# State-space tables moved in program order: all 32 steps beside the four chunks of v

## The chip, the cores and the metric

One core of a Trainium2 chip runs the whole program. The metric is device time in microseconds (us). The kernel before was run three times: 3003.44, 3010.11 and 3009.76 us, median 3009.76 us.

The engines: PE multiplies matrices (PEld loads its weights), DVE and POOL do elementwise work, ACT does activations and copies and issues some DMAs, SP issues most DMAs. Each engine works through one queue in order.

## The reference

Two layers over 256 latent and 256 context tokens of 1024 features. Layer 0 mixes tokens with a gated MLP, layer 1 with a bidirectional diagonal state-space model; after each comes a block of product-key experts. All that matters here lies in the first 400 us, where layer 0's mixer runs:

```python
mod_x = (silu_c @ ada_w[i] + ada_b[i])                    # shift, scale, gate of each sub-layer
xn = _modulate(_rmsnorm(x, norm1_g[i]), sh1, sc1)         # the "first modulated input"
z = jax.nn.gelu(h @ w_in); u, v = jnp.split(z, 2, axis=-1)
v = _layernorm(v, ln_g, ln_b)
v = jnp.einsum("hpq,bnqhd->bnphd", w_s, v) + b_s.T[:, :, None]
return (u * v.reshape(bsz, length, D_MIX)) @ w_out
```

The state-space model of layer 1 needs tables made from its weights alone (powers of the decay times B and C). They don't depend on the tokens, and they are first read in layer 1, after about 1900 us.

## The kernel before

**The opening of layer 0.** `ada_pe(pa, f)` (L187) makes 512 columns of the modulation with 16 matmuls on two loads of 1 MB (`adaw`, two buffers); six calls give shift and scale (calls 0 to 3) and the gate (4 and 5). `start` loads the tokens. `rstd` makes the RMS norm: squares on ACT, sums on DVE, 8 small matmuls, then in `norm_end` a chain of twelve tiny DVE operations (L273 and L244 to L249) that wait for each other, 4 matmuls (L279) and a copy (L281, tile `rr`). `modulate` (L322 to L325) then writes the modulated input as a high part `hh` (ACT) and a low part `hl` (DVE), eight feature blocks one after the other.

**The chunks of v.** `gmlp` loads `cm_w_in` in chunks of 256 columns (`gww`), splits each into `gwh` (ACT) and `gwl` (POOL and DVE), and computes four chunks of v, each with 96 matmuls (L309 to L311) into four PSUM banks that Gelu (L413) empties. After each chunk it calls `vpump()`. After the fourth come `vdone` (it runs the rest of the tables, closes their memory and opens that of what follows), the layer norm of v, and the chunks of u with `wprime_units` (L554, products of the query weights with the keys) and the output product between them.

**The tables.** `s5_units` (L940) is a generator of 32 steps: eight rounds of eight groups each, four steps a round. Steps 1 and 2 belong to B: four DVE multiplications (L952, into tiles `Bd` and `tp`) and one addition (L966), 16 transposes on PE (L973), copies on ACT, two DMAs. Steps 3 and 4 belong to C: four multiplications (L952, into `Cd` and `tp`), one addition (L985), 32 matmuls (L998), copies, DMAs. `go(k)` takes k steps. `Bd` and `tp` have one buffer, `Cd` two.

**What sets the order.** The program is written once in Python; a planner puts every instruction into its engine's queue at the time at which its own model of the machine finds it ready, and among ready ones the one that was written first. So an operation written later can be pulled ahead into time in which its engine would stand idle, if its inputs and its buffers are free. `tc.issue_after(x)` puts what is written in it behind x on x's engine. PSUM banks are tiles named `bk0` to `bk7`, handed out in turn by `bank()` as the program is written; each has one buffer, so the users of a bank follow each other in program order.

The order that is written, before: tables' steps 1 and 2 after `start`; 8 steps after `modulate`; 6 steps behind `modulate`'s last DVE operation; 4 steps after each chunk of v.

Of the kernel before, what the change touches and what calls it, by code (L numbers as in the profile page):

```python
# [71 lines left out]
F1 = 4  # L72
PIN = 1
HA = 50
G_A = 2
G_B = 0
GEND = 0.97
I1 = 0
# [5 lines left out]
WU = (3, 3, 3, 2, 2, 2, 1, 0, 0)  # L84
# [12 lines left out]
AW = (0.12, 0.35)  # L97
PC_ = 1
PD_ = 0
G_C = 8  # L100
G_D = 1
HB = 0
HC = 0
HD = 0
HE = 0
# [6 lines left out]
def tile_hybrid(ctx: ExitStack, tc: tile.TileContext, I, out, stop=None):  # L112
# [11 lines left out]
    def urgent(n):  # L124

        return tc.high_priority(n) if n else ExitStack()

    def use_banks(*b):
        banks[0] = list(b)
# [6 lines left out]
    def pool(name, bufs=1, side=None):  # L136
        return tc.tile_pool(name=name, bufs=bufs, side=side, reuse_waits="tile")
# [21 lines left out]
    def start(pl):  # L159
        load(XT[:, :, 0:SEQ], I["x"].rearrange("(b p) t -> p b t", p=P))  # L160
        for b in range(0, KB, 2):
            pos = pl.tile([P, 2, SEQ], F32, name="pos", bufs=2)
            load(pos, I["pos"][b * P:(b + 2) * P, :].rearrange("(b p) t -> p b t", p=P))
            nc.vector.tensor_add(XT[:, b:b + 2, 0:SEQ], XT[:, b:b + 2, 0:SEQ], pos)
        load(XT[:, :, SEQ:T], I["ctx"].rearrange("(b p) t -> p b t", p=P))
# [3 lines left out]
    r2 = cp.tile([P, T], F32, name="r2")  # L169
# [16 lines left out]
    def ada_pe(pa, f):  # L186

        pm = bank()
        for q in range(2):
            w = pa.tile([P, 4, 512], F32, name="adaw")  # L190
            ends["ada", f] = load(w, I["ada_w0"][q * 512:(q + 1) * 512, f * 512:(f + 1) * 512].rearrange("(b p) f -> p b f", p=P)).ins
            for b in range(4):
                nc.tensor.matmul(pm[0:2, :], cT[:, 4 * q + b, :], w[:, b, :], start=(q + b == 0), stop=(q + b == 4))
        row = pa.tile([2, 512], F32, name="adar")
        nc.scalar.copy(row, pm[0:2, :])
        pm = bank()
        for j in range(4):
            nc.tensor.transpose(pm[:, 2 * j:2 * j + 2], row[:, j * P:(j + 1) * P], ident[0:2, 0:2])
        nc.vector.tensor_tensor(mod[:, 0, 4 * f:4 * f + 4, :],
                                pm[:, 0:8].rearrange("p (j t) -> p j t", t=2),  # L200
                                ab[:, 0, 4 * f:4 * f + 4].unsqueeze(2).to_broadcast([P, 4, 2]), op=OP.add)
        scale_cols(0, 4 * f, 4)
# [81 lines left out]
    def rstd(pl, t0, t1, e=nc.gpsimd):  # L284
        pm = bank()[:, :t1 - t0]
        for b in range(KB):
            norm_add(pl, pm, b, t0, t1, e)
        return norm_end(pl, pm, t1 - t0)
# [3 lines left out]
    def ne(k):  # L292
        return nc.gpsimd if NE[k] == "P" else nc.vector
# [20 lines left out]
    def modulate(pl, r, i, a, sh, parts, keep=None):  # L314

        base, end = parts[0][1], parts[-1][2]
        for b in range(KB):
            u = pl.tile([P, end - base], F32, name="mu", bufs=2)
            for c, t0, t1, hh, hl in parts:
                x = u[:, t0 - base:t1 - base]  # L320
                bias = mod[:, i, sh + b, c:c + 1]
                nc.vector.scalar_tensor_tensor(x, XT[:, b, t0:t1], a[:, i, b, c:c + 1], r[:, t0 - base:t1 - base],  # L322
                                               op0=OP.mult, op1=OP.mult)
                nc.scalar.activation(hh[:, b], x, AF.Identity, bias=bias)
                end_ = nc.vector.scalar_tensor_tensor(hl[:, b], x, bias, hh[:, b].bitcast(F32), op0=OP.add, op1=OP.subtract)  # L325
                if keep is not None:
                    keep(b, c, t0, x, bias)
        return end_.ins
# [923 lines left out]
    def layer0():  # L1252
        n = NDENSE
        low = ExitStack()
        p1 = low.enter_context(pool("h1", side="right"))
        hh1 = p1.tile([P, KB, T], F32R, name="hh1")
        hl1 = p1.tile([P, KB, T], F32R, name="hl1")
# [3 lines left out]
        gw = gws.enter_context(pool("gw", GWB))  # L1261
        with pool("ada0", ADA0) as pa, pool("n1") as pn:
            ada_pe(pa, 0)
            with pool("s5s", side="right") as sm:
                tabs = s5_setup(s5p, sm)
            tables = s5_units(tail.enter_context(pool("s5w", 2, side="right")), *tabs)

            def go(k):
                for _ in range(k):
                    next(tables, None)  # L1270

            ada_pe(pa, 1)
            start(pn)
            go(G_A)
            ada_pe(pa, 2)
            go(G_B)
            with urgent(HA):
                r = rstd(pn, 0, T, ne(0))
            ada_pe(pa, 3)
            with urgent(HB):  # L1280
                end_ = modulate(pn, r, 0, A1, SH1, [(c, t0, t1, hh1[:, :, t0:t1], hl1[:, :, t0:t1]) for c, t0, t1 in PARTS])
            with tc.issue_after(ends["norm"]) if AF_ else ExitStack():
                ada_pe(pa, 4)
                ada_pe(pa, 5)
            go(G_C)
            with tc.issue_after(end_) if G_D else ExitStack():
                go(16 - G_A - G_B - G_C)
        units = []
        ada = []

        def vdone(st):
# [4 lines left out]
            ada.append(ada_rows(pa, [(0, f) for f in range(24, 40)] + LATE[:NP], ada_silu(pa)))  # L1296

        use_banks(*range(7))
        gmlp(gw, hh1, hl1, r2, lambda: go(4), vdone, lambda k: [next(units[0], None) for _ in range(WU[k])], low.close,
             lambda k: [next(g, None) for g in ada for _ in range(k)])  # L1300
        gws.close()
        drain(chain(*ada))
# [3 lines left out]
        with pool("hx") as ph, pool("hold", side="right") as pk, ExitStack() as hold:  # L1306
# [12 lines left out]
            with pool("hc") as pc:  # L1319
# [5 lines left out]
                with pool("n2", side="right") as pn:  # L1325
# [12 lines left out]

                    with urgent(HC):
                        modulate(pn, r2, 0, A2, SH2,  # L1340
# [53 lines left out]
    def layer1():  # L1394
# [20 lines left out]
        with pool("hx1") as ph:  # L1415
# [20 lines left out]
            with pool("de1", 2) as pd, ExitStack() as rs:  # L1436
# [59 lines left out]
                use_banks(*range(8))  # L1496

    layer0()
    if stop in ("gmlp", "peer0"):
        return dump(XT)  # L1500
# [64 lines left out]
```

## Time and profile before

| | |
|---|---|
| median of three runs | 3009.76 us |
| profiled execution, its own time | 2998.49 us |
| its span, first to last instruction | 2996.7 us |
| PE, DVE, ACT, POOL busy | 89%, 77%, 44%, 48% |
| mean granted PE clock | 0.951 |

The profiled execution was 11 us shorter than the median; a span is its own time less 1.8 us. Rows of a timeline give start, duration, engine, line, operation, tiles and count; merged rows give the whole duration of their count. What stands in brackets at the end is the time for which the engine stood idle before, and what released it.

### The profile page before, as it was taken

The numbers are of one execution on the slowest core, as the hardware profiler recorded it, in microseconds if no ns is written. First come the engines' busy times: TensorE is split into PE (matmuls) and PEld (weight loads), VectorE is DVE, ScalarE is ACT, GpSimd is POOL, SyncE is SP. The second block draws the span as 40 slices with busy tenths as digits, with TensorE's granted clock in tenths as the row PEclk, the third lists the DMA queues.
The fourth block names the chain that finished last, engine by engine and source line by source line (L and its number), as shares of the span: only waits on it lengthen the run. The fifth ranks groups of instructions, "written<-read, shape, count | busy, mean of one in ns | idle before, by whom it ended". The sixth has DMA issues, their size and how long they took to land.

```text
span 2996.7 us, 46002 instructions
## 1 busy us (share of the span) xinstructions
PE 2678.1 (89%) x16231; PEld 2375.2 (79%) x16231; DVE 2306.5 (77%) x3980; ACT 1307.0 (44%) x2412; POOL 1438.1 (48%) x1008
## 2 busy tenths in 40 slices
PE   6799899888878888999999987998788889999998
PEld 2599798888766666888888866798787888899997
DVE  7796879999977886999999986464899876644344
ACT  4553243354562233333333323334345665555554
POOL 2031134544634344788888871235454335544443
PEclk8899999999988999999999998999899999999999
DMA  8579743565658787898999987997366778866662
GB/s 276 156 241 338 258 152 123 179 223 191 228 201 268 266 295 255 310 319 311 326 305 316 312 271 253 332 342 204 113 197 232 284 266 297 275 213 216 204 208 104
DMA packets 414576, 738.89 MB, mean 247 GB/s; under 512 B 41604, under 2 KB 272260, under 8 KB 409224
## 3 DMA queue, kind: packets, MB, share of 16 engines
q1 hardware_dynamic: 310240, 507.84, 51.1%
q0 software_dynamic: 36864, 134.23, 13.1%
q10 hardware_dynamic: 67240, 93.88, 8.8%
q8 instruction: 127, 2.08, 0.3%
q14 instruction: 105, 0.86, 0.1%
HBM read 633.07 MB, written 102.77 MB: 246 GB/s over the span
## 4 chain that ended last, share of the span: by engine, by line
PE 31%; DMA 13%; DVE 11%; issue 7%; POOL 5%; ACT 1%; SPq 1%; DVEq 0%; ACTq 0%; POOLq 0%
PE bk L756 6%; PE bk L757 5%; PE bk L755 5%; PE bk L311 4%; PE bk L309 4%; PE bk L310 4%; DMA vr<-peer_v 3%; DMA row<-peer_v,ids 2%; POOL row L601 2%; DMA row<-peer_u,ids 2%; DVE ul L303 1%; POOL ul L303 1%; POOL vl L303 1%; PE bk L554 1%; SPq L134 1%
## 5 line engine op out<-in xcount | busy, mean ns | idle before, releaser
L311 PE MATMUL bk<-hxh,ul 128*128 128x384 f32 (+1 forms) x2048 | 649.5, 318 | 47.7 <-DVE ul L303 28.5
L309 PE MATMUL bk<-hxh,uh 128*128 128x384 f32 (+1 forms) x2048 | 649.6, 317 | 11.7 <-ACT uh L301 6.9
L310 PE MATMUL bk<-hxl,uh 128*128 128x384 f32 (+1 forms) x2048 | 643.8, 314 | 0.0
L303 POOL TENSOR_TENSOR ul<-ur,uh 128x512 fp32r<-128x512 f32 x299 | 447.1, 1501 | 301.9 <-ACT uh L301 268.7
L303 POOL TENSOR_TENSOR vl<-vr,vh 128x512 fp32r<-128x512 f32 x256 | 363.0, 1422 | 461.1 <-ACT vh L301 454.6
L756 PE MATMUL bk<-vl,wh 128*128 128x512 f32 x1280 | 517.8, 405 | 63.6 <-POOL vl L303 46.1
L755 PE MATMUL bk<-vh,wh 128*128 128x512 f32 x1280 | 511.5, 400 | 36.8 <-ACT wh L301 19.5
L301 ACT ACTIVATE vh<-vr 128x512 fp32r<-128x512 f32 x512 | 315.4, 623 | 519.2 <-DMA vr<-peer_v 375.9
L757 PE MATMUL bk<-vh,wl 128*128 128x512 f32 x1280 | 509.0, 398 | 0.0
L301 ACT ACTIVATE uh<-ur 128x512 fp32r<-128x512 f32 x512 | 315.5, 629 | 408.4 <-PE bk L310 226.6
L311 PEld LDWEIGHTS bk<-hxh,ul 128*128 128x128 f32 x2048 | 397.5, 194 | 55.5 <-DVE ul L303 33.8
L309 PEld LDWEIGHTS bk<-hxh,uh 128*128 128x128 f32 x2048 | 398.3, 194 | 18.9 <-ACT uh L301 7.9
L310 PEld LDWEIGHTS bk<-hxl,uh 128*128 128x128 f32 x2048 | 398.2, 194 | 5.0
L303 DVE TENSOR_TENSOR wl<-w,wh 128x384 fp32r<-128x384 f32 (+1 forms) x256 | 192.6, 753 | 242.0 <-ACT wh L301 241.4
L756 PEld LDWEIGHTS bk<-vl,wh 128*128 128x128 f32 x1280 | 246.8, 193 | 135.3 <-POOL vl L303 62.4
L755 PEld LDWEIGHTS bk<-vh,wh 128*128 128x128 f32 x1280 | 246.5, 193 | 92.0 <-ACT vh L301 22.7
L757 PEld LDWEIGHTS bk<-vh,wl 128*128 128x128 f32 x1280 | 247.1, 193 | 50.7 <-DVE wl L303 0.3
L303 DVE TENSOR_TENSOR vl<-vr,vh 128x512 fp32r<-128x512 f32 x256 | 205.2, 812 | 74.4 <-ACT vh L301 73.5
L624 DVE SCALAR_TENSOR_TENSOR acc<-row,wts,acc 128x1024 f32<-128x1024 f32 x127 | 208.3, 1640 | 21.2 <-DMA row<-peer_v,ids 20.1
L611 DVE SCALAR_TENSOR_TENSOR gscr<-row,hn 128x1024 f16<-128x1024 f32 x128 | 209.7, 1639 | 18.3 <-DMA row<-peer_u,ids 17.1
L303 DVE TENSOR_TENSOR ul<-ur,uh 128x512 fp32r<-128x512 f32 x213 | 188.7, 888 | 43.5 <-ACT uh L301 41.7
L223 DVE SCALAR_TENSOR_TENSOR adasv<-adatv,cB 128x1024 f16<-128x1024 f32 x112 | 157.3, 1405 | 61.0 <-DMA adatv<-ada_t 60.1
(325 smaller groups left out, 4966.1 us busy)
## 6 DMA issues: line engine op xcount, KB each, us to landing
ur<-peer_ut SPq DMA_DIRECT2D x256, 512.0 KB
vr<-peer_v SPq DMA_DIRECT2D x256, 512.0 KB
gd<-Gs ACTq DMA_DIRECT2D x40, 1024.0 KB
adatv<-ada_t SPq DMA_DIRECT2D x72, 512.0 KB
wqT<-peer_w_q SPq DMA_DIRECT2D x64, 512.0 KB
Gr<-gd SPq DMA_DIRECT2D x120, 192.0 KB
wp<-wpo ACTq DMA_DIRECT2D x32, 512.0 KB
wpi<-wp SPq DMA_DIRECT2D x16, 1024.0 KB
```

Source lines behind the costliest of these rows:

```text
L223: e.scalar_tensor_tensor(scr, w, 1.0, cB[:, t], op0=OP.mult, op1=OP.mult, accum_out=mod[:, i, f, t:t + 1])
L301: nc.scalar.activation(hi, src, AF.Copy)
L303: return e.tensor_tensor(lo, src, hi.bitcast(F32), op=OP.subtract)
L309: nc.tensor.matmul(o, ah, bh, start=(i == 0), stop=False)
L310: nc.tensor.matmul(o, ah, bl, start=False, stop=False)
L311: last = nc.tensor.matmul(o, al, bh, start=False, stop=(i == n - 1))
L601: tc.keep_in_program_order(nc.gpsimd.indirect_dma_start(out=r[:], out_offset=None, in_=I[f"peer_{table}{i}"], in_offset=bass.IndirectOffse ...
L611: nc.vector.scalar_tensor_tensor(scr, r, 1.0, hn, op0=OP.mult, op1=OP.mult, accum_out=dots[:, h, k:k + 1])
L624: nc.vector.scalar_tensor_tensor(acc, r, w, acc, op0=OP.mult, op1=OP.add)
L755: nc.tensor.matmul(o, wh[:, js], vh, start=first, stop=False)
L756: nc.tensor.matmul(o, wh[:, js], vl, start=False, stop=False)
L757: nc.tensor.matmul(o, wl[:, js], vh, start=False, stop=last)
```

## The change

The constants take all steps out of the opening, and `vpump()` takes eight steps instead of four. The block behind `modulate`'s last operation stays but takes none.

```diff
-G_A = 2
+G_A = 0
 G_B = 0
...
-G_C = 8
+G_C = 0
 G_D = 1
 HB = 0
+NT0 = 0
...
             go(G_C)
             with tc.issue_after(end_) if G_D else ExitStack():
-                go(16 - G_A - G_B - G_C)
+                go(NT0)
...
-        gmlp(gw, hh1, hl1, r2, lambda: go(4), vdone, ...
+        gmlp(gw, hh1, hl1, r2, lambda: go(8), vdone, ...
```

The number of steps (32) and what each computes stay the same. Since `bank()` counts on as the program is written, the opening and the first chunk get other banks than before: round 0's B transposes now use bk4, bk5, bk6 and bk0, and the first chunk of v uses bk0 to bk3. From the end of the tables on the banks are the same as before.

## Rows read from the trace of the kernel before

**Rows 1.** The page, its first line.
```profile
span 2996.7 us, 46002 instructions
```

**Rows 2.** Windows: us, busy us of PE, PEld, DVE, ACT, POOL, clock, DMA share, GB/s.
```profile
36.00:48.00 12.00, 7.90 (x32) 3.27 (x32) 11.58 (x10) 7.06 (x16) 6.75 (x4) 0.86 1.06 345
...
37.40:199.70 162.30, 129.44 (x825) 99.50 (x826) 145.60 (x145) 82.38 (x196) 31.67 (x15) 0.88 0.63 196
...
103.00:112.00 9.00, 2.42 (x12) 2.43 (x13) 8.93 (x8) 2.38 (x6) 0.00 (x0) 0.50 0.62 164
...
128.10:198.70 70.60, 69.43 (x560) 67.68 (x560) 66.94 (x49) 40.94 (x96) 17.63 (x9) 0.98 0.60 181
...
206.10:361.00 154.90, 154.49 (x962) 136.60 (x960) 112.10 (x215) 44.93 (x80) 29.14 (x19) 1.00 0.91 313
```

**Rows 3.** Table operations on DVE: count, ns min/median/max, first and last start.
```profile
L952 DVE TENSOR_TENSOR tp<-c,YC x16: 1201/1218/1226, 56.5 to 195.7; 128x1024 f32<-128x1024 f32 x16
...
L966 DVE TENSOR_TENSOR Bd<-Bd,tp x8: 2279/2292/3272, 50.9 to 192.2; 128x2048 f32<-128x2048 f32 x8
```

**Rows 4.** Timeline of DVE, from the first table operation to the last.
```profile
37.45 2.35 DVE L952 TENSOR_TENSOR Bd<-b,YB 128x1024 f32<-128x1024 f32 x2
...
41.99 8.90 DVE L952 TENSOR_TENSOR Cd<-c,YC 128x1024 f32<-128x1024 f32 x4
50.81 0.15 DVE L273 TENSOR_SCALAR dr<-bk 128x4 f32<-128x4 f32 x1
50.88 3.27 DVE L966 TENSOR_TENSOR Bd<-Bd,tp 128x2048 f32<-128x2048 f32 x1
...
73.05 2.36 DVE L952 TENSOR_TENSOR tp<-b,YB 128x1024 f32<-128x1024 f32 x2
...
75.90 0.16 DVE L249 SCALAR_TENSOR_TENSOR vr<-yr,vr 128x4 f32<-128x4 f32 x1
85.31 1.67 DVE L322 SCALAR_TENSOR_TENSOR mu<-XT,A,rr 128x256 f32<-128x256 f32 x4 [9.24 <-ACT rr L281]
...
100.03 2.35 DVE L952 TENSOR_TENSOR Bd<-b,YB 128x1024 f32<-128x1024 f32 x2
102.30 0.48 DVE L325 SCALAR_TENSOR_TENSOR hl<-mu,mod,hh 128x256 fp32r<-128x256 f32 x1
...
187.66 4.55 DVE L952 TENSOR_TENSOR Bd<-b,YB 128x1024 f32<-128x1024 f32 x2
...
197.51 2.28 DVE L985 TENSOR_TENSOR Cd<-Cd,tp 128x2048 f32<-128x2048 f32 x1
```

**Rows 5.** Timeline of SP's DMA queue, around 31 us.
```profile
31.00 0.50 SPq L134 DMA_DIRECT2D b<-s_b  x1
...
33.43 2.18 SPq L134 DMA_DIRECT2D gww<-cm_w_in  x2
```

**Rows 6.** Timeline of PE: chunk 0 of v, and the end of the tables.
```profile
58.34 2.15 PE L193 MATMUL bk<-adaw,cT 128*2 128x512 f32 x3 [0.46 <-ACT BTq L975]
...
83.49 1.16 PE L279 MATMUL bk<-ident,vr 128*128 128x128 f32 x8
...
109.58 3.67 PE L973 MATMUL bk<-ident,Bd 128*128 128x128 f32 x16 [10.00 <-DVE Bd L966]
114.39 5.77 PE L998 MATMUL bk<-Cd,bdg 128*48 128x144 f32 x32 [1.14 <-DVE Cd L985]
...
128.13 0.58 PE L309 MATMUL bk<-gwh,hh 128*128 128x256 f32 x1 [4.93 <-ACT BTq L975]
...
198.81 1.91 PE L973 MATMUL bk<-ident,Bd 128*128 128x128 f32 x16
200.65 4.12 PE L998 MATMUL bk<-Cd,bdg 128*48 128x144 f32 x32
204.71 1.98 PE L420 MATMUL bk<-wsT,ones 128*128 128x512 f32 x4
...
217.73 0.61 PE L554 MATMUL bk<-kT,wqT 128*128 128x128 f32 x4
```

More of the change, by code (lines that the diff above doesn't have):

```diff
@@ L1298, in layer0 @@
         use_banks(*range(7))
-        gmlp(gw, hh1, hl1, r2, lambda: go(4), vdone, lambda k: [next(units[0], None) for _ in range(WU[k])], low.close,
+        gmlp(gw, hh1, hl1, r2, lambda: go(8), vdone, lambda k: [next(units[0], None) for _ in range(WU[k])], low.close,
              lambda k: [next(g, None) for g in ada for _ in range(k)])
```

## The prediction

> **What bounds the kernel now.** I read the summary first, for the span [rows 1], then windows of the opening [rows 2], because the change touches nothing behind it. Two stages stand out. From 206.1 to 361.0 us PE is busy 154.49 of 154.90 us at full clock: whatever ends this stage earlier or later is PE's own work, and the stage begins when the tables are done (chunk 0 of u, then the first product L554 at 217.73 [rows 6]). Ahead of it, from the first table operation at 37.45 to the end of the last at 199.7 (197.51 + 2.28 [rows 4]), DVE is busy 145.6 of 162.3 us [rows 2]. So DVE is what carries the opening: 16.7 us of idle time is all that a better order could take out of it. PE idles more there, but for DVE: it waits 10.00 us for `Bd` at 109.58, and starts chunk 0 of v only at 128.13, although the last piece of its input was written at 102.8 (102.30 + 0.48) [rows 4, 6]. This is the gap at which the change aims, and the first thing to see is that PE isn't the engine that is late there.
>
> **The change part by part.**
>
> *The work itself.* A B half of a round is four multiplications (two back to back take 2.35 us [rows 4]) and one addition (2.29 [rows 3]), together 7.0 us; a C half is the same. A round costs 14.0 us, eight rounds 112 us. None of it goes away. PE needs 1.91 + 4.12 us a round and about 11.6 us a chunk of v (an estimate: a chunk has as many columns as chunk 0 of u, which runs from 206.1 to 217.7 [rows 2, 6]), so 23.7 us for a chunk with its two rounds, under DVE's 28. DVE stays the bound.
>
> *What can still be pulled ahead.* The planner may pull tables ahead of chunk 0 as it does now. What stops it is PSUM: a bank's users follow each other as written. That this holds shows at 58.34: call 3 of `ada_pe` waited for `BTq`, the copy that empties bk4 from round 0's transposes [rows 6]. With the new count round 0's fourth transposes use bk0, which chunk 0 of v holds first. Until that is emptied `Bd` stays taken, so no more than this runs early: round 0 (14.0 us), the first two multiplications of round 1's C (2.35) and the two of its B that go to `tp` (2.35), 18.7 us. Before, rounds 0 and 1 and four multiplications of round 2 (at 73.05 and 100.03) had run by 102.8: 28.0 + 4.7 = 32.7 us. So 14.0 us of tables move from before the modulated input to behind it.
>
> *When the modulated input is ready.* The weights of chunks 0 and 1 of v (two DMAs of 1 MB) now stand ahead of the loads of B and C, which SP issued first before [rows 5]. At 345 GB/s [rows 2] that is 6.1 us; `Bd` began at 37.45 for another reason (its table was being made), so I take 4.5 of 0 to 6.1: tables begin at 42.0. The chain of the norm begins at 50.81 behind eight multiplications and ends at 76.1, since the planner puts table operations between its tiny ones [rows 4]. I assume that it does so again with what is left: 18.7 us, plus 5.2 for operations beside POOL's splits (four multiplications took 8.90 instead of 4.7, one addition 3.27 instead of 2.29 [rows 3, 4]), plus twelve links at 0.2 (2.4), plus some 2.5 for DVE's share of the splits and modulation: 42.0 + 28.8 = 70.8. PE's broadcast (1.16 [rows 6]) and the copy add 1.8 if PE isn't behind a load, as it was before (it finished at 84.65, 8.6 us after the chain). `modulate` took 17.5 us with two table multiplications inside, so 15.1 without. Ready at 87.7 instead of 102.8.
>
> *From there to the end of the tables.* Before: 199.7 - 102.8 = 96.9 us. Added: the 14.0 moved; a hand-over in which DVE has nothing, since chunk 0 must end, be emptied, and round 0's last transposes follow before `Bd` is free (nearest row: PE's 4.93 us wait for such a copy [rows 6]; bounds 2 to 12, the upper one a whole chunk; I take 5); one more chunk's split by POOL beside DVE, for chunk 1 of u, whose buffer now comes free earlier (two multiplications took 4.55 instead of 2.35, at 187.66; twice that is 4.4). Taken away: DVE's waits between 128.1 and 198.7, 70.6 - 66.94 = 3.7 us, because PE there was full with one round a chunk, and now has slack. Sum 116.6, so the tables end at 204.3, 4.6 us later than before.
>
> *The hand-over to PE's stage.* Before, from 199.7 to the first product at 217.7, PE ran 4.1 of round 7's products, 1.4 of L420 and 11.6 of chunk 0 of u. Chunk 3 of v is now done long before, so L420 and the first half of u (5.8; its bank is free once round 7's B is copied) run while DVE makes the last C. That gives back 7.2 us (bounds 0 to 13; the second half's bank waits for round 7's C). What follows is PE's gapless 143 us with its loads released by the same tables.
>
> *The sum.* +4.6 - 7.2 = -2.6 us at 361, and nothing behind hides or multiplies it. On the profiled execution's own time (span plus 1.8) that is 2995.9; that execution lies 11.3 us under the median of the three runs, so against the median: 3009.8 - 2.6 = 3007 us. A single measurement of this kernel can't tell less than 0.3% (9 us) from no change; so this is no change, with a slight lean to faster.
>
> **The rivals.**
>
> *The chain runs ahead (faster).* If B and C land so late that the planner puts the norm's chain in front of the tables, the modulated input is ready near 75 and DVE's idle time shrinks. For it: the chain alone costs 2.4 us, and the tables start later than before, while the sums under the chain don't depend on them. Against it: the planner fills every gap of a chain with whatever is ready [rows 4]. The gain is bounded by DVE: begun at 42.0 with 145.6 of work and 4.4 more of collision, without a gap, the tables end at 192.0, 7.7 earlier; with the 7.2 of PE's hand-over, 14.9, and 19 if B and C land as early as before. I take 17: 2993 us.
>
> *PE makes DVE wait (slower).* The one mechanism that ends on the other side: in PE's queue the transposes of a round stand behind a chunk of v that was written earlier, and `Bd` has one buffer. From Bd's addition on DVE has the C half (7.0) and two multiplications (2.35) to do, 9.3 us; PE needs a chunk and the transposes, 11.6 + 1.9 = 13.5. Each chunk that falls so costs 4.2 us, four cost 17. For it: chunk 0 certainly falls so, and PE made DVE wait before too [rows 2]. Against: only some banks couple, and a chunk may also fall into DVE's C half. It decides the sign from two such chunks on. 3007 + 16 = 3023 us.
>
> *The clock (slower).* Between 103 and 112 us PE worked 2.42 of 9.00 us, the granted clock was 0.50 (the level of 1.2 GHz), and 16 transposes then took 3.67 us against 1.91 at full clock; 32 products took 5.77 against 4.12 [rows 2, 6]. With the new order PE works about 23.7 of 33 us. If it fell to the lower level in every stage, a chunk would take 23.2 and two rounds 18.9, 42.1 us against DVE's 28 + 5; 9 us too many in each of four stages, of which the first is covered, so +27: 3034 us. Against it: the low stretch followed a wait of 10 us, and the waits to come are shorter; over the whole opening PE was busy 129.44 of 162.3 us, in uneven pieces, and the clock was 0.88 [rows 2]. The Trainium skill has the rule for it ("TensorE: Matmul & The Clock Gate", section "HAM oscillation — how this bites in real kernels"): a PE that waits between bursts drops to the lower clock and pays at each burst anew; the window at 103 to 112 agrees, and by the rule alone this rival would be the forecast, at 3034.
>
> *It doesn't do what it says.* The planner pulls the same operations ahead in another order, and all stays: 3010 us. Against it are the banks; for it, that 32.7 us were pulled ahead before.
>
> **How the numbers follow.** Forecast 0.37, chain ahead 0.27, PE makes DVE wait 0.20, clock 0.08, nothing 0.08. The forecast's own range is 3007 plus or minus 9 (hand-over 2 to 12, PE's gain 0 to 13, start 0 to 6). Faster by over 0.3% (under 3000.7): most of the chain's case and a tail of the forecast, 0.30. Slower (over 3018.8): most of the two slower cases and a small tail, 0.25. Within: 0.45. The range takes in both signs: from 2990 (the chain's case with an early start) to 3026 (four chunks that make DVE wait); left out are the clock's case and the outer tails, 0.2.
>
> **What would show it.** In the profile after: the last `hl` at about 88 us instead of 102.8, with no L998 ahead of it; chunk 0 of v from about 75 to 91 instead of 128; the last L985 ending at about 204; L420 and half of u ahead of the last L998; the first L554 near 215; PE without a gap until about 358. DVE's idle time between 42 and 204 near 13 us. It is wrong if the tables end before 196 or after 212, if `hl` is written before 78 or after 97, or if the granted clock between 100 and 200 stays under 0.9.

## The result and the profile after

The changed kernel takes 3034.1 us (median of 6 runs, 3024.7 to 3043.2) where the kernel before, run beside it, takes 3010.8 (3003.4 to 3014.6): a ratio of 1.0079, 95% interval 1.0054 to 1.0103. It is slower by some 24 us; the forecast was 3007. The profiled execution took 3024.7 us. Lines of the changed kernel are one higher than before (L952 is now L953, L554 is L555).

The page's first line, and windows of the opening (columns as in [rows 2]):

```profile
span 3023.0 us, 45994 instructions
...
41.80:217.50 175.70, 127.90 (x812) 100.97 (x810) 151.58 (x160) 83.65 (x197) 38.44 (x19) 0.87 0.58 180
88.90:100.50 11.60, 11.60 (x87) 9.74 (x86) 1.59 (x6) 4.61 (x9) 0.04 (x1) 1.00 0.17 47
100.00:200.00 100.00, 76.83 (x576) 73.44 (x575) 94.32 (x73) 54.71 (x133) 19.22 (x10) 0.90 0.56 168
100.50:217.50 117.00, 84.58 (x624) 80.46 (x622) 111.32 (x95) 63.31 (x152) 27.20 (x13) 0.87 0.57 172
...
240.00:384.90 144.90, 142.70 (x908) 126.90 (x907) 105.06 (x160) 40.09 (x73) 28.33 (x18) 1.00 0.89 302
```

The first window runs from the first table operation to the last. DVE is busy 151.6 of 175.7 us there, idle 24.1, where it was busy 145.6 of 162.3 [rows 2], idle 16.7. The second window is the hole: PE is busy for all of its 11.6 us, DVE for 1.6.

DVE's timeline, to be read against [rows 4]:

```profile
41.76 3.42 DVE L953 TENSOR_TENSOR Bd<-b,YB 128x1024 f32<-128x1024 f32 x2
...
75.96 1.67 DVE L323 SCALAR_TENSOR_TENSOR mu<-XT,A,rr 128x256 f32<-128x256 f32 x4 [8.35 <-ACT rr L282]
...
87.24 1.66 DVE L326 SCALAR_TENSOR_TENSOR hl<-mu,mod,hh 128x256 fp32r<-128x256 f32 x4
94.33 0.17 DVE L200 TENSOR_TENSOR mod<-bk,ab 128x8 f32<-128x8 f32 x1 [5.43 <-PE bk L199]
...
99.84 0.69 DVE L304 TENSOR_TENSOR gwl<-gww,gwh 128x512 fp32r<-128x512 f32 x1 [4.11 <-ACT gwh L302]
100.45 3.43 DVE L953 TENSOR_TENSOR Bd<-b,YB 128x1024 f32<-128x1024 f32 x2
...
210.46 2.27 DVE L967 TENSOR_TENSOR Bd<-Bd,tp 128x2048 f32<-128x2048 f32 x1
...
212.79 2.34 DVE L953 TENSOR_TENSOR tp<-c,YC 128x1024 f32<-128x1024 f32 x2
...
215.19 2.27 DVE L986 TENSOR_TENSOR Cd<-Cd,tp 128x2048 f32<-128x2048 f32 x1
```

The last piece of the modulated input is written at 88.9 instead of 102.8, 14 us earlier, as the change means it. The next multiplication starts at 100.45, and the last table operation ends at 217.46 instead of 199.79. PE's timeline, against [rows 6]:

```profile
74.15 1.16 PE L280 MATMUL bk<-ident,vr 128*128 128x128 f32 x8
...
78.76 0.39 PE L310 MATMUL bk<-gwh,hh 128*128 128x256 f32 x1
...
98.71 1.47 PE L974 MATMUL bk<-ident,Bd 128*128 128x128 f32 x12
100.11 4.12 PE L999 MATMUL bk<-Cd,bdg 128*48 128x144 f32 x32
...
107.89 1.94 PE L974 MATMUL bk<-ident,Bd 128*128 128x128 f32 x16 [3.66 <-DVE Bd L967]
...
140.95 3.29 PE L974 MATMUL bk<-ident,Bd 128*128 128x128 f32 x16 [5.06 <-DVE Bd L967]
...
176.80 3.65 PE L974 MATMUL bk<-ident,Bd 128*128 128x128 f32 x16 [8.97 <-DVE Bd L967]
...
212.88 3.65 PE L974 MATMUL bk<-ident,Bd 128*128 128x128 f32 x16 [8.37 <-DVE ve L245]
217.41 3.78 PE L421 MATMUL bk<-wsT,ones 128*128 128x512 f32 x4 [0.89 <-ACT BTq L976]
220.21 1.42 PE L310 MATMUL bk<-hh,gwh 128*128 128x512 f32 x1
...
225.39 4.12 PE L999 MATMUL bk<-Cd,bdg 128*48 128x144 f32 x32
...
237.01 0.60 PE L555 MATMUL bk<-kT,wqT 128*128 128x128 f32 x4
239.75 0.50 PE L310 MATMUL bk<-hh,gwh 128*128 128x512 f32 x1 [2.14 <-ACT uT L376]
```

Chunk 0 of v starts at 78.8 instead of 128.1, and with its weights and input at hand PE runs it to the end at 98.9, between calls of `ada_pe`, before it transposes the other twelve blocks of round 0. From then on each second round is waited for: 3.7, 5.1, 9.0 and 8.4 us, 26.1 in all (the releaser shown for the last is a small operation behind `Bd`'s addition on DVE). So from 100.5 to the tables' end it is PE that waits for DVE: PE is busy 84.6 of 117.0 us, DVE 111.3. The first product of PE's long stage comes at 237.0 instead of 217.7, and the first product of the next norm (L267 before) at 386.5 instead of 361.7. That shift of 24.8 us is nearly the whole loss: at the end of the program it is 26.3. It has two parts: 17.7 us by which the tables end later, and 7.1 from there to the next norm (169.0 us instead of 161.9).

### The profile page after: what moved, and what is told of

Read it like the earlier page. It is cut to its first block, busy times and chain, and to the rows that moved or that the text cites. A ratio compares the mean times of both kernels' runs of the same rounds, so it can differ in the third digit from the quotient of the medians.

```text
span 3023.0 us, 45994 instructions
## 1 busy us (share of the span) xinstructions
PE 2689.2 (89%) x16231; PEld 2385.4 (79%) x16231; DVE 2305.7 (76%) x3980; ACT 1307.7 (43%) x2412; POOL 1449.9 (48%) x1008
## 4 chain that ended last, share of the span: by engine, by line
PE 28%; DMA 15%; DVE 13%; issue 7%; POOL 4%; SPq 1%; ACT 1%; DVEq 0%; ACTq 0%; POOLq 0%
PE bk L757 5%; PE bk L758 5%; PE bk L756 5%; DMA vr<-peer_v 4%; PE bk L310 4%; PE bk L312 4%; PE bk L311 4%; DMA row<-peer_v,ids 3%; POOL row L602 2%; DMA Gr<-gd 2%; SPq L135 1%; DVE ul L304 1%; DMA row<-peer_u,ids 1%; PE bk L555 1%; DVE w L742 1%
## 5 line engine op out<-in xcount | busy, mean ns | idle before, releaser
L612 DVE SCALAR_TENSOR_TENSOR gscr<-row,hn 128x1024 f16<-128x1024 f32 x128 | 201.0, 1570 | 12.3 <-DMA row<-peer_u,ids 11.1
```

The costliest lines, as they stand in the source:

```text
L612: nc.vector.scalar_tensor_tensor(scr, r, 1.0, hn, op0=OP.mult, op1=OP.mult, accum_out=dots[:, h, k:k + 1])
```

## The experiments

Theory 1: `Bd` has one buffer, and the transposes that free it stand behind a whole chunk of v in PE's queue. Theory 2, formed on the way: PE is as much the bound as DVE once chunk 0 has begun, and it is only without a gap if each chunk (11.7 us) is followed by one round (6.0), not by two. The rival to both is the forecast's own view, that DVE's work alone sets the end.

The ratios are to runs of the kernel before, made beside each on the same chip. The columns from the third on are times in us in the one profiled execution: end of the last `hl`, end of the last table operation, first product of the long stage, first product of the next norm.

| kernel | ratio to before (95%) | hl | tables | L554 | next norm |
|---|---|---|---|---|---|
| before | 1 | 102.8 | 199.8 | 217.7 | 361.7 |
| changed | 1.0079 (1.0054 to 1.0103) | 88.9 | 217.5 | 237.0 | 386.5 |
| e1, two steps behind each bank | 1.0051 (1.0032 to 1.0069) | 88.6 | 215.0 | 236.8 | 382.0 |
| e2, two Bd | 1.0004 (0.9988 to 1.0021) | 96.6 | 201.5 | 219.0 | 363.1 |
| e3, 8 ahead, held behind hl | 1.0018 (1.0007 to 1.0030) | 63.8 | 202.2 | 228.6 | 373.2 |
| e4, v's split on DVE | 1.0048 (1.0028 to 1.0068) | 81.8 | 209.1 | 230.0 | 375.9 |
| e5, before, two Bd | 0.9985 (0.9969 to 1.0002) | 103.2 | 195.9 | 217.1 | 361.6 |
| e6, before, split on DVE | 0.9943 (0.9925 to 0.9961) | 94.5 | 188.0 | 206.7 | 351.6 |
| e7, 8 ahead, free | 1.0014 (0.9999 to 1.0028) | 98.0 | 196.8 | 227.0 | 372.7 |
| e8, before, both | 0.9977 (0.9961 to 0.9994) | 106.3 | 196.2 | 218.2 | 362.7 |
| e9, 2 steps put back | 0.9993 (0.9975 to 1.0010) | 100.6 | 208.3 | 233.5 | 373.2 |
| e10, 16 held, 4 per chunk | 0.9968 (0.9947 to 0.9988) | 64.7 | 199.0 | 217.1 | 360.8 |
| e11, before, 8 per chunk | 1.0047 (1.0026 to 1.0068) | 103.7 | 198.0 | 237.5 | 384.5 |
| e12, two Bd and split | 0.9999 (0.9979 to 1.0020) | 90.6 | 200.2 | 219.8 | 373.0 |
| e13, last wait filled | 1.0057 (1.0040 to 1.0075) | 90.3 | 219.6 | 238.6 | 382.5 |
| e14, as e10, split on DVE | 0.9989 (0.9973 to 1.0005) | 62.3 | 194.3 | 212.9 | 356.4 |

The last column and the ratio go together: 3010 us times (ratio - 1), less the shift of the last column, lies between -13.6 and +2.0 in the fifteen rows, 5.5 low on average, since the profiled execution of before was one of the short ones. So a difference of 20 us in the last column is the time's; one of 5 is not told apart by the time.

**e1.** The steps spread over a chunk's banks.

```diff
-                vpump()                    # behind a chunk, go(8)
+                    vpump()                # behind each of its four banks, go(2)
```

> The changed kernel with the same 32 steps behind the chunks of v, but two of them issued after each of a chunk's four banks instead of eight after the fourth. Theory 1 (one Bd buffer, and the transposes that free it stand behind a whole chunk in PE's queue): DVE's idle time between the last hl and the next multiplication of a round falls from 11.5 us to under 4, PE's waits for Bd between the chunks (3.7, 5.1, 9.0 and 8.4 us) fall by more than half, the last L986 ends at 204 to 209 instead of 217.4, and the time falls by 8 to 13 us against the changed kernel, to 3021 to 3026. Rival (DVE is the bound by its own work: multiplications at half speed beside POOL and the layernorm's small operations between them; the waits only move): the last L986 ends after 214 and the time stays within 4 us of 3034.

DVE's idle time behind `hl` fell to 6.4 us, but the tables end at 215.0, only 2.5 earlier. PE's waits for `Bd` fell to 3.2 us, and it waited 10.2 for `Cd` and 10.0 for `BTq` instead. The time, 3023.2, is where theory 1 put it, but that is 0.3% under the changed kernel with intervals that overlap, and the steps that should lead there didn't come. So the place behind a whole chunk is not the cause by itself: most of the waits moved, as the rival had it.

**e2.** A second `Bd`.

```diff
-TB = dict(Bd=1, BTq=2, Cd=2, wk=2)
+TB = dict(Bd=2, BTq=2, Cd=2, wk=2)
...
-            u = pl.tile([P, end - base], F32, name="mu", bufs=2)
+            u = pl.tile([P, end - base], F32, name="mu", tag="sq" if i == 0 and a is A1 and end - base == T else "mu", bufs=2)
...
-            r = pl.tile([P, n], F32, name="rr")
+            r = pl.tile([P, n], F32, name="rr", tag="sqs" if n == T else "rr")
```

> The changed kernel with two Bd buffers instead of one (room for it is made by letting mu and rr of the first norm take the places of sq and sqs, which are dead by then). Theory 1 (single Bd): round 1's multiplications start within 3 us of the last hl instead of 11.5, DVE waits for Bd no more between the chunks, the last L986 ends at 204 to 209, time 3021 to 3026. Rival (what keeps DVE is the order of PE's queue alone: the transposes come as late as before, a second buffer is filled and then waited for too): the first wait goes but comes back a round later, last L986 after 213, time within 4 us of 3034.

DVE's timeline of e2, and PE's:

```profile
53.60 2.35 DVE L953 TENSOR_TENSOR Bd<-b,YB 128x1024 f32<-128x1024 f32 x2
...
96.14 0.47 DVE L326 SCALAR_TENSOR_TENSOR hl<-mu,mod,hh 128x256 fp32r<-128x256 f32 x1
...
102.29 3.43 DVE L953 TENSOR_TENSOR Bd<-b,YB 128x1024 f32<-128x1024 f32 x2
```

```profile
100.55 1.47 PE L974 MATMUL bk<-ident,Bd 128*128 128x128 f32 x12
101.95 4.12 PE L999 MATMUL bk<-Cd,bdg 128*48 128x144 f32 x32
106.00 1.97 PE L974 MATMUL bk<-ident,Bd 128*128 128x128 f32 x16
```

Round 0's transposes come as late as in the changed kernel (100.55), but round 1's B was begun at 53.60 in the second buffer and is transposed at 106.00 without a wait. DVE is still without table work for 5.7 us behind `hl`, more than expected, and the loss is gone all the same: tables to 201.5, time level with before. Of PE's waits for `Bd` 1.4 us are left, beside 4.8 for a C half and 10.5 for the copies into `BTq` (6.4 in the changed kernel). What the second buffer mends, by these rows, is that DVE and PE need not meet once per round.

**e3 and e7.** Eight of the 32 steps ahead of chunk 0 again, in two ways.

```diff
-NT0 = 0          # e3
+NT0 = 8
```
```diff
-G_C = 0          # e7
+G_C = 8
```

> The changed kernel with the first 8 steps (two rounds) issued ahead of chunk 0 of v, the other 24 behind chunks 0, 1 and 2, none behind chunk 3. Theory 1: the transposes of round 0 don't stand behind chunk 0, so the 11.5 us of DVE's idle time behind the last hl are gone; hl is some 4 us later, the last L986 ends at 205 to 210, and with nothing queued behind chunk 3 the time is 3018 to 3026. Rival (the place behind chunk 0 is not what costs; DVE's own work is): last L986 after 214, time within 4 us of 3034.

> The changed kernel with one of its three edits undone: 8 steps stand ahead of chunk 0 again, not held behind the last hl, and 24 behind chunks 0 to 2. Theory 1: both first rounds' transposes stand ahead of chunk 0, so DVE goes from hl to the next multiplication in under 3 us, as in the kernel before; the last L986 ends at 198 to 206 and the time is 3005 to 3014, as much as 8 ahead behind hl or better. Rival (what costs is that the tables are spread over the chunks, eight steps behind each): still over 3020.

In e3 I overlooked that this place is held behind the last `hl` (`issue_after(end_)` in the diff): no table ran ahead of `hl`, which was therefore written at 63.8, 25 us earlier than in the changed kernel, not 4 later. Both kernels have the hand-over mended (0 and 1.2 us) and the tables end at 202 and 197, about where before ended them, but the next norm begins 11 us late in both (e7's time, 3016.2, came out 2 us above what was expected, e3's, 3013.1, 5 us below): PE has the last part of chunk 3 to do when the tables are done (it ends at 215.8 and 214.3), because two rounds stand behind each of the chunks 0 to 2. That DVE's end and PE's start of the long stage come apart is what theory 2 was formed on.

**e4 and e6.** v's subtractions all on DVE, in the changed kernel and in the one before.

```diff
-                wh, wl = weights(I["cm_w_in"], f, (1, 2))
+                wh, wl = weights(I["cm_w_in"], f, (1, 0))
```

> The changed kernel with all gwl subtractions of v's chunks on DVE (split 1:0 instead of 1:1 with POOL). In the changed kernel the multiplications beside POOL's bursts take 13.7 us more than the others from 100 to 217; 11 subtractions of 0.6 us come to DVE instead. If DVE's own work sets the end of the tables, it comes 7 us earlier (near 210) and the time is 3025 to 3029. If the waits for Bd set it (theory 1), DVE only waits longer, the last L986 stays after 214, time within 4 us of 3034.

> The kernel before with all gwl subtractions of v's chunks on DVE. DVE is its bound up to 199.7 and idles 8 us after the last hl; the multiplications beside POOL's bursts take 13.2 us longer there, and 11 subtractions of 0.6 us come to DVE. If DVE's work sets the end of the tables there, 5 to 9 us faster: 2999 to 3005. Rival (POOL's bursts lie where DVE would wait for PE anyway): 3008 to 3011.

What POOL costs DVE, in the changed kernel (POOL's timeline, then DVE's beside it):

```profile
199.85 8.17 POOL L304 TENSOR_TENSOR gwl<-gww,gwh 128x512 fp32r<-128x512 f32 x4 [26.49 <-ACT gwh L302]
237.74 4.99 POOL L304 TENSOR_TENSOR gwl<-gww,gwh 128x512 fp32r<-128x512 f32 x4 [29.71 <-ACT gwh L302]
```

```profile
200.48 4.22 DVE L953 TENSOR_TENSOR Bd<-b,YB 128x1024 f32<-128x1024 f32 x2
204.63 4.48 DVE L953 TENSOR_TENSOR tp<-b,YB 128x1024 f32<-128x1024 f32 x2
```

Beside POOL's four subtractions a pair of multiplications takes 4.2 to 4.5 us instead of 2.35 [rows 4], and POOL's four take 8.17 where four with no table operation beside them take 4.99 (at 237.74). Together they take 9.3 us, from 199.85 to 209.11, nearly the 9.7 that they would take one after the other. The Trainium skill says so ("SBUF — State Buffer", section "SBUF: two separate sides"): the pair of ports that VectorE and GpSimd share is locked for a whole instruction, and the other engine waits; these rows agree. With the split on DVE the changed kernel's tables end at 209.1, as expected (its time, 3020.4, is lower than that), though 7 us of the 8.4 come from an earlier `hl`. Only 2.2 of these are a shorter chain of the norm (it ends at 64.9 instead of 67.1), without POOL's first burst beside it. The rest is PE's broadcast, which runs at 67.05 instead of 74.15: the products of `ada_pe` ahead of it in PE's queue waited 1.7 us for their weights instead of 5.2. The kernel before gains most (windows, then PE's timeline in both, e6 first, and DVE's in e6):

```profile
37.00:188.00 151.00, 124.40 (x823) 98.13 (x824) 140.16 (x158) 83.47 (x196) 7.94 (x4) 0.93 0.68 211
128.10:189.70 61.60, 61.08 (x506) 59.29 (x505) 59.25 (x58) 39.38 (x93) 8.56 (x5) 1.00 0.60 180
```

```profile
66.20 7.03 PE L193 MATMUL bk<-adaw,cT 128*2 128x512 f32 x16 [0.77 <-DMA adaw<-ada_w]
...
75.53 1.06 PE L279 MATMUL bk<-ident,vr 128*128 128x128 f32 x8
```

```profile
73.85 5.07 PE L193 MATMUL bk<-adaw,cT 128*2 128x512 f32 x8 [4.23 <-DMA adaw<-ada_w]
```

```profile
77.58 1.67 DVE L322 SCALAR_TENSOR_TENSOR mu<-XT,A,rr 128x256 f32<-128x256 f32 x4 [2.24 <-ACT rr L281]
```

In these windows of e6, DVE is busy 140.2 us up to the end of the tables instead of 145.6 with more instructions, PE is full from 128 on, and the whole stage is 11 us earlier at L554 and 10 at the next norm, more than the 5 to 9 expected. Only half of it is DVE's shorter work (5.4 us less busy); the other half is 5.9 us less idle, mostly because the broadcast runs at 75.53 instead of 83.49 [rows 6] and DVE waits 2.2 us for it instead of 9.2 [rows 4]. At 0.9943 this is the fastest of all versions.

**e5 and e8.** The same two edits in the kernel before: two `Bd`, and both together.

> The kernel before with two Bd buffers, edited as in the changed kernel with two. Theory 1 (the single Bd buffer costs where a round's transposes stand behind a chunk of v that is itself late; the kernel before had round 0 and 1 transposed ahead of the chunks): DVE idles only 8.0 us between the last hl and the end of the tables there, of which 3 to 5 us are waits for a buffer, so the gain is at most 5 us: 3003 to 3010. Rival (a second buffer helps wherever it is put, and the changed kernel with it came out level only because two things cancel): 22 us faster here too, near 2987.

> The kernel before with two Bd buffers and the subtractions of v's chunks on DVE, the candidate to beat both. If waits and work at half speed beside POOL add up: the tables end 8 to 14 us earlier than 199.7, 2996 to 3003. If PE's chunk of v and its banks take over as the bound of the stretch: within 4 us of the better of the two alone.

A second `Bd` ends the tables 3.9 us earlier there and moves L554 by 0.6: PE was full from 128 on, so an earlier end on DVE is worth nothing. The time, 3008.5, is in the range of theory 1, though DVE's idle time there was 5.5 us before (96.9 less 91.4) and not the 8.0 of the expectation. This is the control for e2: the second buffer is worth something only where one buffer holds the engines up. Both edits together do neither of what was expected and are no better than the split alone (L554 at 218.2 against 206.7): the planner fills the second buffer ahead of the modulation, the broadcast runs at 83.99 instead of 75.53, `hl` comes 12 us later than in e6, and PE waits 21.6 us for `Cd` ahead of chunk 0.

**e9.** Two of the 32 steps put back.

```diff
-G_A = 0
+G_A = 2
```

> The changed kernel with 2 of its 32 steps put back where they stood: the B half of round 0 is issued ahead of call 2 of ada_pe, all else as changed. Theory 1 (Bd stays taken until round 0's transposes, which stand behind chunk 0 of v on bank 0): these transposes now run before chunk 0, so DVE goes on with round 1 while it waits for the norm's broadcast and behind the last hl; the 11.5 us of idle time behind hl fall under 6, the last L986 ends at 205 to 211, the time falls by 6 to 12 us against the changed kernel, to 3023 to 3029. Rival (the place of round 0 is not what costs): tables end after 214, time within 4 us of 3034.

PE's timeline of e9, and DVE's:

```profile
55.31 3.68 PE L974 MATMUL bk<-ident,Bd 128*128 128x128 f32 x16 [9.85 <-DVE Bd L967]
...
91.33 0.39 PE L310 MATMUL bk<-gwh,hh 128*128 128x256 f32 x1
```

```profile
37.47 2.35 DVE L953 TENSOR_TENSOR Bd<-b,YB 128x1024 f32<-128x1024 f32 x2
...
109.33 4.02 DVE L953 TENSOR_TENSOR Cd<-c,YC 128x1024 f32<-128x1024 f32 x2 [0.47 <-PE bk L999]
```

All 16 transposes of round 0 run at 55.3, ahead of chunk 0 at 91.3, and the tables begin at 37.5 again. The tables end at 208.3, in the range expected; the 7.3 us of idle time behind `hl` are more than expected (two of the three waits are for chunk 0's copies and for weights). The time is level with before, a gain of 0.86% on the changed kernel, larger than the 13.3 us that the trace shows in its last column; with both intervals 13 us is just possible. So where round 0 stands is a part of the loss, as theory 1 had it: the tables end 9 us earlier although `hl` comes 11.7 us later, and eight steps still stand behind each chunk.

**e10 and e11.** One round per chunk in the changed kernel, two in the kernel before.

```diff
-NT0 = 0                                   # e10, on the changed kernel
+NT0 = 16
-        gmlp(gw, hh1, hl1, r2, lambda: go(8), vdone, ...
+        gmlp(gw, hh1, hl1, r2, lambda: go(4), vdone, ...
```
```diff
-        gmlp(gw, hh1, hl1, r2, lambda: go(4), vdone, ...   # e11, on the kernel before
+        gmlp(gw, hh1, hl1, r2, lambda: go(8), vdone, ...
```

> The changed kernel with 16 steps ahead of chunk 0 as in the kernel before, but all of them held behind the last hl, and 4 (one round) behind each chunk. With 8 steps held, hl was written by 63.8 and the tables ended at 202.2, but PE had chunk 3 and then u left, since two rounds stood behind each chunk. Theory 2 (PE is as much the bound as DVE from chunk 0 on, and it is only gapless with one round, 6.0 us, per chunk of 11.7): DVE ends the tables at 190 to 198, PE runs chunks 0 to 3 and rounds 4 to 7 back to back, L555 begins at 207 to 214, the time is 3000 to 3008. Rival (starting all tables behind hl throws away 26 us of DVE at the start, which nothing gives back): tables end after 205, time 3015 or more.

> The kernel before with 8 steps behind each chunk instead of 4: 16 ahead, 8 behind chunks 0 and 1, none behind 2 and 3. Theory 2: DVE's tables end 2 to 6 us earlier than 199.7, since it no longer waits for a full PE, but PE waits 8 to 12 us for Bd in two places and has chunks 2 and 3 to do afterwards, so L554 comes 5 to 12 us later than 217.7 and the time is 3015 to 3023. Rival (DVE alone is the bound, as the forecast had it): the end of the tables and with it L554 come earlier, time 3004 to 3010.

e11 first, a window and PE's timeline:

```profile
161.60:224.70 63.10, 56.13 (x433) 54.81 (x434) 42.84 (x61) 29.97 (x69) 11.30 (x7) 0.92 0.69 213
```

```profile
161.61 3.24 PE L973 MATMUL bk<-ident,Bd 128*128 128x128 f32 x16 [8.59 <-DVE Bd L966]
...
193.48 3.65 PE L973 MATMUL bk<-ident,Bd 128*128 128x128 f32 x16 [5.65 <-DVE Bd L966]
...
237.48 2.73 PE L554 MATMUL bk<-kT,wqT 128*128 128x128 f32 x23
```

Nothing else of the change is in this kernel: its `hl` is where it was, its tables end 1.8 us *earlier*, and still L554 comes 19.8 us later (more than the 5 to 12 expected) and the program takes 0.47% longer (3026.6 us, above the range expected). In the window PE is busy 56.1 of 63.1 us: it waits for the second round of a pair and has nearly all of chunk 2 and all of chunk 3 to do when the tables are done. And e10, in which no table stands ahead of the modulation, as in the change, but one round behind each chunk (the first 16 steps then stand ahead of chunk 0, so two things differ from the changed kernel):

```profile
63.60:199.00 135.40, 110.65 (x766) 93.59 (x765) 124.61 (x96) 69.22 (x165) 17.73 (x9) 0.91 0.58 174
126.80:360.50 233.70, 231.44 (x1572) 210.67 (x1572) 189.12 (x293) 92.56 (x191) 52.71 (x32) 0.99 0.81 269
```

DVE starts its tables 27 us later than before and ends them at 199.0, a little behind what was expected; from chunk 0 at 126.8 on PE is busy 231.4 of 233.7 us; L555 at 217.1 (later than the 207 to 214 expected) and the next norm at 360.8 are those of the kernel before.

The pair shows that two rounds behind a chunk lose time by themselves, and that an opening without tables does not. It doesn't show that their number carries the whole loss of the changed kernel: e11 loses with tables that end early and a PE that is left with two chunks, the changed kernel with tables that end 17.7 us late and all chunks done by 198.7. The table above shows both ways. From the end of the tables to the next norm it is 161.9 us before and 162 to 167 in the other kernels with four steps behind a chunk, all of which end their tables by 200. With eight, either the tables end late (at 208 to 220: the change, e1, e4, e9, e13) or PE has more left (171 to 187 us: e3, e7, e11, e12); e2 alone shows neither. No run alters the number of rounds in the changed kernel and nothing else (16 steps would have to stand elsewhere), so its share of the 24.8 us is not shown.

**e12.** The changed kernel with two `Bd` and the split on DVE.

> The changed kernel with two Bd buffers and the subtractions of v's chunks on DVE: both costs that the runs so far found in it taken away. With two buffers alone it came level with the kernel before, with the split alone 9 us faster than as changed. If the two add up: tables end near 193, L555 near 211, time 2996 to 3002, level with the kernel before with the split on DVE (2996). If the second buffer leaves DVE no idle time that the split could fill (or PE takes over): 3004 to 3010.

Its time is level with before (3011.6, just above the second range) and no better than the second buffer alone; its trace comes to the next norm 11 us late, like those of e3, e7 and e9. PE waits 5.2, 9.0 and 2.7 us for `Bd` again: the two don't add. Why the second buffer doesn't loosen the engines here as in e2 stays open.

**e13.** PE's last wait filled, everything else in its place.

```diff
+                if half == 1 and q in FILL:      # FILL = {6: 15}
+                    pf = ps.tile([P, 512], F32, name="bk7")
+                    for k in range(FILL[q]):
+                        nc.tensor.matmul(pf, ident, Cd[:, 0].rearrange("p g s c -> p (g s c)")[:, 0:512], start=True, stop=True)
```

> The changed kernel with 15 products added that nothing reads (a tile of the identity by Cd, 128x512, into the eighth bank), in PE's queue behind the products of round 6, where PE stands idle for 8.4 us before the last round's transposes; every other instruction keeps its place. It asks how much of the lost hand-over is the granted clock: after that wait the 16 transposes took 3.65 us instead of 1.91 and the four L421 3.78 instead of 1.98. Theory (the clock costs what these rows show and no more): the transposes take 1.9 and the four L421 2.0, the first L555 comes 3 to 5 us earlier than 237.0, the end of the tables stays within 1.5 us, and the time falls by 2 to 6 us, which these rounds can hardly tell from nothing. Rival (the clock is most of the 24 us): first L555 before 230, time 3022 or less. If the order is all that counts: first L555 within 1.5 us of 237.0.

```profile
206.71 13.14 PE L1011 MATMUL bk<-Cd,ident 128*128 128x512 f32 x30
219.68 1.91 PE L975 MATMUL bk<-ident,Bd 128*128 128x128 f32 x16
221.52 4.12 PE L1000 MATMUL bk<-Cd,bdg 128*48 128x144 f32 x32
225.57 1.98 PE L422 MATMUL bk<-wsT,ones 128*128 128x512 f32 x4
```

I sized the filler wrong: a product of this shape counts as two in the trace (15 written, 30 recorded), so it ran 13.1 us where 8 were wanted and held the transposes up by some 5 (`Bd` was added at 214.9). The first L555 comes later, not earlier, than in the changed kernel. But PE runs at full clock (granted clock 1.00 from 219.6 to 227.5; in the changed kernel 0.50, the level of 1.2 GHz, from 212.8 to 222.2, behind its wait), the transposes take 1.91 and the four L421 1.98, and no wait follows before the next norm: from the end of the tables to the next norm's first product it is 162.9 us, against 169.0 in the changed kernel and 161.9 before. So at this place the lower clock and the waits behind it are some 6 us of the 24.8, and not most of it. The time, 1.0057 against 1.0079, is 6.6 us lower, with intervals that overlap.

**e14.** e10 with the split on DVE.

> The kernel with 16 steps held behind the last hl and one round per chunk, with the subtractions of v's chunks on DVE. Held back alone the time was 0.32% under the kernel before and PE was gapless from 126.8; the split alone gave 0.57% on the kernel before. In the held kernel the multiplications beside POOL take 11.2 us more than the others. If DVE sets the start of chunk 0 (rounds 0 to 3, then PE without a gap): the tables' part under POOL is small before chunk 0, so DVE is relieved only where PE is full, L555 begins at 212 to 217 and the time is 2997 to 3003. If both gains add: L555 at 205 to 209, time 2985 to 2992.

The opening is 4.4 us shorter than e10's, as the first theory had it, and the time can't be told from either e10 or before: the split is worth most where it lets chunk 0 begin earlier, as in e6 (117.7 instead of 128.1), and less here (123.9 instead of 126.8), where PE is full behind that.

## Why the prediction was wrong

Its sum was -2.6 us at the end of the long stage; the profile has +24.1 there (384.9 against 360.8). Step by step:

**The start.** "Tables begin at 42.0": 41.76. The number was right, the reason at best in part: only one of the two loads of the chunks' weights stood ahead of B and C in SP's queue (B was issued at 32.67 instead of 31.00), and the first six links of the norm's chain ran ahead of the first multiplication, which followed them without idle time. With two steps back in front (e9) the tables begin at 37.5.

**What can be pulled ahead.** "18.7 us": exactly these operations ran ahead of `hl`, two of the four multiplications and no more of round 1's B, and no L999. The list was right; the bank that chunk 0 shares with the fourth group of transposes explains it only in part, since twelve of round 0's sixteen transposes ran behind chunk 0, and not four.

**The modulated input.** "Ready at 87.7": 88.9. The parts were off and cancelled: the norm's chain ended at 67 us instead of 70.8, and PE's broadcast waited to 74.15 behind products of `ada_pe` that had waited 5.2 us for their weights.

**The hand-over of DVE.** "A hand-over in which DVE has nothing ... bounds 2 to 12 ... I take 5": 11.6, close to the upper bound (6.6 of the error). I let PE go from chunk 0 straight to one last group of transposes. When `hl` was done PE still had more than half of chunk 0 to do, to 98.9, and then twelve transposes, which end at 100.18. Small operations that wait for chunk 0's stretch (L200 at 94.33, the `gwl` at 99.84) stood ahead in DVE's queue too, but the multiplication begins 0.3 us after the transposes, so they cost no more than that.

**PE's slack.** "Taken away: DVE's waits between 128.1 and 198.7 ... because PE there was full with one round a chunk, and now has slack": this step failed in kind. From 100.5 on DVE idles 5.7 us (117.0 less 111.3), as much as before (5.5 of 96.9), so nothing was taken away; with 1.5 us more work than I had counted, that is 5.4 us. PE did have slack in sum, 32.4 us, but DVE's short waits for it (2.6 us behind L999) and for ACT's copies (2.9) stayed. The fact behind it stood in the prediction, and I drew the wrong side from it: PE was busy 69.4 of 70.6 us there [rows 2], so it was the bound of that stretch, and its order, one round to one chunk, was what kept it full. "DVE stays the bound" held up to the tables' end, but it compared sums (23.7 against 28 us for a chunk and two rounds) and not the order in which the two engines meet: with one `Bd` PE can transpose the second round only when DVE has made it, 3.7 to 9.0 us after the first round's products, and meanwhile nothing else stands next in its queue. e11 shows the number of rounds alone at +0.47%, e10 an opening without tables and one round behind each chunk at -0.32%, and e2 the change level with before once a second buffer loosens the two engines.

**The gift at PE's hand-over.** "L420 and the first half of u ... gives back 7.2 us (bounds 0 to 13)": from the tables' end to the end of the long stage it took 6.4 more than before, outside the bounds, the largest single error (13.6). L421 shares its banks with round 7's transposes, which wait for `Bd`'s last addition at 212.7; that is 4.7 us before the tables end, not the 7.0 of a C half, because the planner had done the other half of C's multiplications earlier. After the wait of 8.4 us PE was at the lower clock (granted 0.50; 16 transposes 3.65 us, four L421 3.78). So L421 began at 217.41, with the tables' end, and four short waits follow behind it. e13 brings these 6 us back by keeping PE at work.

In sum, from the forecast: -2.6; `hl` +1.2, hand-over +6.6, no slack +5.4 (tables end 13.2 later than 204.3), PE's hand-over +13.6: 24.2. Against the kernel before, the 17.7 us by which the tables end later are 4.3 of a later start, 7.4 more of idle time and 6.0 more of busy time on DVE.

**The rivals.** "PE makes DVE wait" (3023, a chance of 0.20) came nearest in place and size, but with half of the pair: it saw DVE held up by PE's chunks and priced 4.2 us for each, and what the trace shows is PE held up by DVE's second round, 26.1 us in four waits. e1 shows that taking the transposes from behind the chunk doesn't mend it. "The clock" gave 3034 and the time came out there, for another reason: between 100 and 200 us the granted clock is 0.90, as in the kernel before and in e9, and no chunk took the 23.2 us it was built on (chunk 3 ran from 181.3 to 198.7 with a round's 4.1 us of products inside). Behind the waits at 140.95, 176.80 and 212.88 the transposes took 3.29, 3.65 and 3.65 us instead of 1.91, with a granted clock of 0.58, 0.50 and 0.50; behind the shortest, at 107.89, they took 1.94 at 1.00. By the rule of the Trainium skill named there ("TensorE: Matmul & The Clock Gate", section "HAM oscillation — how this bites in real kernels"), a burst behind a wait is paid at the lower clock: the first three rows agree, the fourth doesn't. What the last of them cost, with the waits behind it, is some 6 us by e13. "The chain runs ahead" came true in part, unasked for, in e3, e10 and e14: `hl` at 62 to 65. By itself it gained nothing on the kernel before (e3, +0.18%), since PE then has part of chunk 3 left. "It doesn't do what it says" was wrong.

Not settled: how the 24.8 us divide between round 0's place, the single buffer and the number of rounds; why the time of e9 gained more than its trace shows; and why e14, 4.4 us shorter in the opening, isn't faster than e10. What follows the next norm's first product, which no kernel here changes, takes 2632 to 2649 us in the sixteen profiles, so a few us in the opening are easily hidden.

## What to carry to other kernels

Where two engines take turns over a single buffer, compare them in the order of their queues, not by their sums: two rounds queued behind each chunk left PE waiting for the second one, though PE had less to do than DVE. An input that is ready earlier helps only if nothing else then holds the engine that reads it: PE began chunk 0 49 us earlier here and then waited 26.1 us for DVE. And before moving work between stages, look who slows whom where it is: an engine that was given "spare" work beside DVE cost more here than the work was worth.

## What the runs showed that I had not expected

Giving eleven more subtractions of 0.6 us to DVE, the busiest engine of the opening, made the kernel before 0.57% faster (0.39 to 0.75): with POOL busy for 7.9 us instead of 31.7, DVE's busy time up to the end of the tables *fell* from 145.6 us of 162.3 to 140.2 of 151.0. The other half of the gain came from a place at which nobody aimed, PE's broadcast of the norm, which came 8 us earlier because the weights of `ada_pe`'s products ahead of it did. And holding the tables back by 27 us at the start (e10) cost nothing against the kernel before, since the norm and the modulation, without tables between their steps, end 38 us earlier (64.7 against 102.8).
